# Writing out TensorE's order in the stage of four recurrent heads, with scans for window sums and a last tile in two pieces

## The chip, the core and the metric

The kernel runs on one core of one Trainium2 chip. The core has a matrix engine (TensorE, PE in the profile; PEld are its weight loads), a vector engine (VectorE, DVE), an activation engine (ScalarE, ACT), GpSimd (POOL) and SyncE (SP), which here only issues DMAs. Each engine works through its own queue in order, and engines wait for each other by semaphores. The metric is the time of one execution in microseconds (us), smaller is better. The kernel before takes 1327.94 us, the median of 3 runs (1326.75 to 1328.4).

## The reference, cut to what matters

One layer of a decoder trunk on 1024 tokens plus 16 meta tokens (L = 1040 rows) of width 1024, all in float32:

```python
u = rmsnorm(h, mix_norm_pre)
q, f_logit, i_in, g_out, v_pool, gate_a, gate_b = split(u @ w_in)
a = hgrn2(q, f_logit, i_in, g_out, lbs, hgrn_out_norm)      # 4 heads, key and value width 128
p = multiscale_pool(v_pool, pool_proj, pool_scale)          # 4 groups, windows 2, 4, 8, 16
z = sigmoid(gate_a) * (a @ w_branch_hgrn) + sigmoid(gate_b) * (p @ w_branch_pool)
h = h + rmsnorm(z @ w_out, mix_norm_post)
u = rmsnorm(h, ffn_norm_pre)
gt = causal_dwconv(u @ ffn_w_gate, ffn_conv_w, ffn_conv_b)
h = h + rmsnorm((gelu(gt) * (u @ ffn_w_up)) @ ffn_w_down, ffn_norm_post)
```

`hgrn2` is a linear recurrence per head: a state of 128 x 128 decays by a forget gate f for each key channel, takes in k times v, and is read by q. Its output is normalised per head by its root mean square, multiplied by a gain and by sigmoid(g). `multiscale_pool` takes, per group of 128 channels, the mean over the last w rows, less the row itself, through a 128 x 128 matrix and a scale.

## The kernel before, in words

Matmuls are done in three passes: each operand is split into a high and a low part (`hi`, `lo`: ACT rounds to fp32r, DVE subtracts), and high by high, low by high and high by low are summed. Splits are thus a large part of the work of ACT and DVE.

The stages in order of time: norms and the transposed features `uhi`/`ulo` (two large tiles, `ubig`, line 431); value and first gate projections; a Strassen stage for the logits f, for q and for the two branch gates, which go to DRAM; **the stage of the heads** (about 326 to 580 us), which the change is about; the output projection (`Mixer`); the gated MLP, again by Strassen; and the down projection with its own one-level Strassen scheme, whose last quarter of products is summed tile by tile at the end (lines 1725 to 1745).

The stage of the heads is described by the string `ORDER` (line 56). Its words are, in the order in which the program emits the work:

- `h0` to `h3`: the next step of that head's generator `head_steps` (line 650). A head has twelve steps. They are: load f, q, kb and k from DRAM; a block step (32-wide blocks on the diagonal, PE name `sb`, then the first growth); six levels 2, 4, ... 64 (PE name `sl`); the transposes of k (`pt`), ahead of which the head's values `vh` are loaded; the state chain (`ds`, then seven dependent DVE operations `st`); the output (`po`), its square and the split of the square (`rh` on ACT, `rl` on DVE); and the mean-square step (`ms`: a matmul with ones, then Ln and Exp on ACT, and two products on DVE with the gain and the gate `sg`).
- A level consists of small matmuls that read k and q, then `grow`, in which DVE multiplies halves of k and q by f in place, then a masked copy into `near` or copies by ACT into `sc`. The next level's matmuls need the grown k and q, and growth has to wait for the matmuls that read the old ones.
- `PV0` to `PV3` and `G2`, `G3`: projections of the features with 8 k (blocks of 128 input rows) in three chunks of columns, for the pool and for two output gates. `PVa1` and `PVb1` are the first and second half of `PV1`. `post_pv` copies the banks to `vp` and sums the windows by doubling: adds of the row and the row 1, 2, 4, 8 back (line 817), 1 + 2 + 3 + 4 = 10 adds for the four groups.
- `sp`: `pool_split`, which finishes the mean and splits it. `PP`: one k, the group's 128 x 128 matrix; `post_pp` writes `phi` (ACT) and `plo` (DVE).
- `BB0` to `BB7`, `BA0` to `BA7`: the branch projections of the pool and of the heads, 4 k each (PE names `pbb` and `pba`), multiplied by the gates loaded from DRAM (`sa`). `BB` reads all four `phi`/`plo`; `BA` reads all four heads' split outputs, which `sa` makes.
- `w0` to `w5`: weights of the MLP are loaded, split and stored to DRAM for later (`keep`, lines 911 to 931; DVE at lines 920 and 923).

A projection holds three PSUM banks from its first matmul until its results are copied out; there are eight banks. Most tiles of the stage live in 26 slots (`slot`, pool `fm`). Weights come through three raw buffers. DMAs on SP are issued in the order of the queue, and `issue_after` keeps a load behind an earlier one.

What sets the order: outside blocks marked `tc.manual_schedule(engines=...)`, a planner simulates the program when it is built and places each engine's instructions by the simulated times and by their place in the program. In such a block the engines that are named keep the written order. The loop over `ORDER` (lines 1139 to 1178) is in no such block: the planner orders all engines there, PE too, so what PE does in the profile is not the string word by word.

Of the kernel before, what the change touches and what calls it, by code (L numbers as in the profile page):

```python
# [14 lines left out]
P = 128  # L15
D = 1024
SEQ = 1024
NM = 16
# [48 lines left out]
def trunk_kernel(ctx: ExitStack, tc: tile.TileContext, x, meta_tokens, mix_norm_pre,  # L67
# [124 lines left out]
    def proj_parts(w, col, n_k, xs, chunks, ws=None, name="pj", by_bank=0):  # L192
# [5 lines left out]
        for k in range(n_k - by_bank):  # L198
            if 0 < k == n_k // 2:
                yield banks  # L200
# [449 lines left out]
    def head_steps(h):  # L650
# [70 lines left out]
        for lv in LEVELS:  # L721
            if lv == NM:
                pm = bank("sm")
                for i in range(HALO):
                    pe.matmul(pm[:NM, i : i + 1], k[:, i * NM : (i + 1) * NM], q[:, NM + T0 + i : NM + T0 + i + 1],
                              start=True, stop=True)
                act.copy(scm, pm[:NM, :HALO])
# [8 lines left out]
        heads[h]["v"] = slot(NCH * P, name="vh")  # L736
        vmeta = small([NM, P], "vmeta", "vmeta", 2)
        with tc.issue_after(stage["load"].ins):
            nc.sync.dma_start(vmeta, vmd[:, h * P : (h + 1) * P])
            nc.sync.dma_start(heads[h]["v"].rearrange("p (c v) -> p c v", c=NCH),  # L740
                              vd[:, :, h * P : (h + 1) * P].rearrange("c p v -> p c v"))
# [47 lines left out]
        rh, rl = split(rs, "r", eng(f"rsl.{h}"))  # L789
        yield  # L790
# [6 lines left out]
        dve.scalar_tensor_tensor(o, o, ong[:, h : h + 1], rs, ALU.mult, ALU.mult)  # L797
        eng(f"osg.{h}").tensor_tensor(o, o, sgs[h], ALU.mult)
# [6 lines left out]
    def post_pv(g, pv):  # L805
        w = POOL_WINDOWS[g]
        vp, s1 = slot(L, name="vp"), slot(L, name="s1")
        s2 = slot(L, name="s2") if w > 2 else None
        for (lo, n), ps in zip(CH_ALL, pv):
            act.copy(vp[:, lo : lo + n], ps[:, :n])  # L810
        cur, step = vp, 1
        bufs = [s1, s2]
        while step < w:
            nxt = bufs[0]
            bufs = bufs[::-1]
            a = 2 * step - 1
            dve.tensor_tensor(nxt[:, a:L], cur[:, a:L], cur[:, a - step : L - step], ALU.add)
            cur, step = nxt, 2 * step
        pooled[g] = (cur, vp)

    def pool_split(g):
        w = POOL_WINDOWS[g]
        cur, vp = pooled[g]
        if w > T0 + 1:

            c1 = small([P, 1], "c1", "c1", 2)
            dve.tensor_reduce(c1, vp[:, 0 : T0 + 1], mybir.AxisListType.X, ALU.add)
            dve.tensor_scalar(cur[:, T0 : T0 + 1], c1, float(w) / (T0 + 1), None, ALU.mult)
# [9 lines left out]
    def post_pp(g, pp):  # L838
        a, b_ = slot(TQ, F32R, "phi"), slot(TQ, F32R, "plo")
# [276 lines left out]
    jobs_ = [(k.rstrip("a"), i) for k, i in order if k[0].isupper() and k[-1] != "b"]  # L1116
# [22 lines left out]
    for kind, i in order:  # L1139
        if kind == "sp":  # L1140
            pool_split(i)
            continue
        if kind == "w":
            keep_first(i) if i < EARLY else next(keeps[i - EARLY])
            continue
        if kind == "sa":
            ahl[i] = split(heads[i]["o"], "a")
            continue
        if kind == "h":
            if i not in gens:  # L1150
                gens[i] = head_steps(i)
            next(gens[i], None)
            continue
        kind, part = kind.rstrip("ab"), kind[-1]
        src, n_k, xs, chunks, post = job(kind, i)
        if part == "b":
            banks = next(halves_of[kind, i])
# [3 lines left out]
            continue  # L1161
        if kind in ("BA", "BB"):
            load_gate(sas if kind == "BA" else sbs, kind == "BB", i)
        ws = loader.next()
        if (kind, i) == ("BA", KD - 1):
            z0 = [split_z(0, k) for k in range(ZA)]
        if part == "a":
            halves_of[kind, i] = proj_parts(None, 0, n_k, xs, chunks, ws=ws, name="p" + kind.lower())
            next(halves_of[kind, i])
            continue  # L1170
        banks = proj(None, 0, n_k, xs, chunks, ws=ws, name="p" + kind.lower(),
                     by_bank=2 if (kind, i) == ("BA", KD - 1) else 0)
        loader.ahead()
        pay()
        after[kind, i] = post(banks)
        if kind == "BA":
            dve.tensor_tensor(sas[i], sas[i], sbs[i], ALU.add)
            z[i] = sas[i]
# [546 lines left out]
    banks = [bank("pd") for _ in range(NT)]  # L1725
    for n, k in enumerate(range(KT, KH)):
        if n == 0:
            prep_last(KH - 2, False)
            for t in range(NT):
# [10 lines left out]
    for t in range(NT):  # L1740
        for j in range(KT):
# [34 lines left out]
```

## Time and profile before

| | before |
|---|---|
| median of 3 runs | 1327.94 us (1326.75 to 1328.4) |
| the profiled execution | 1327.77 us, its span 1326.0 us |
| mean granted clock of TensorE | 0.989 |
| ACT busy | 524.2 us (40%) |
| POOL busy | 356.7 us (27%) |

The profile was taken from one execution. Busy times are the unions of an engine's instructions; matmuls are pipelined and overlap, so the spacing of their starts, not the listed duration, tells what one costs. `x` counts instructions. The number in brackets behind an instruction is the idle time of its engine before it, and after `<-` what released it. In a group by line, the figures after `|` are the busy time in us and the mean in ns, then the idle time before. In a stretch, the last three columns are the granted clock of TensorE (1.00 is full speed), the share of the 16 DMA engines and GB/s.

### The profile page before, as it was taken

The page shows a single profiled execution, that of the slowest core. Times are in us where ns is not written, and L with a number is a line of the kernel's source. Part 1 is how long each engine was busy: PE and PEld are TensorE (multiplying, and loading weights), DVE is VectorE, ACT ScalarE, POOL GpSimd, SP SyncE. Part 2 cuts the span into 40 slices and gives each one's busy share as a digit, 9 for nine tenths or more (in the row PEclk, how much of TensorE's full clock was granted, in tenths as well). Part 3 has the DMA queues.
Part 4 walks back from the last instruction along what each step waited for, and adds up shares of the span by engine and source line. Part 5 has one row for each costly group of instructions (what it writes and reads, how often), then busy time and mean ns, then how long its engine had stood idle before and what let it go on. Part 6 is the DMA issues. An engine that isn't in the chain of part 4 may idle for free.

```text
span 1326.0 us, 21946 instructions
## 1 busy us (share of the span) xinstructions
PE 1292.2 (97%) x8617; PEld 1144.3 (86%) x8617; DVE 964.4 (73%) x1297; ACT 524.2 (40%) x903; POOL 356.7 (27%) x303
## 2 busy tenths in 40 slices
PE   8999999999988889999999999999999999999997
PEld 7799899999988789987898888888888888888886
DVE  6768965444677866775578999888998885455757
ACT  5554533333137444235564322222222233444443
POOL 3015333220000000061025555545555652000000
PEclk9999999999989989999999999999999999999999
DMA  7135643334341276887686677677767799666644
GB/s 273 42 106 175 198 147 104 112 109 144 121 151 49 79 248 230 311 279 258 229 286 234 180 208 191 191 207 176 174 157 165 162 250 304 216 223 222 222 174 159
DMA packets 143802, 247.62 MB, mean 187 GB/s; under 512 B 11000, under 2 KB 75164, under 8 KB 143698
## 3 DMA queue, kind: packets, MB, share of 16 engines
q1 hardware_dynamic: 131634, 221.83, 49.4%
q0 software_dynamic: 12064, 24.38, 11.0%
q8 instruction: 68, 1.11, 0.3%
q14 instruction: 36, 0.29, 0.1%
HBM read 174.11 MB, written 95.09 MB: 203 GB/s over the span
## 4 chain that ended last, share of the span: by engine, by line
PE 94%; issue 2%; ACT 2%; DMA 1%; DVE 1%; SPq 0%; DVEq 0%; ACTq 0%
PE P L303 17%; PE P L304 17%; PE P L306 17%; PE pd L183 5%; PE pd L184 5%; PE pd L185 5%; PE pm L183 2%; PE pm L184 2%; PE pm L185 2%; PE pbb L203 1%; PE pbb L204 1%; PE pbb L207 1%; PE pba L203 1%; PE pv L184 1%; PE pba L204 1%
## 5 line engine op out<-in xcount | busy, mean ns | idle before, releaser
L304 PE MATMUL P<-v,whi 128*128 128x512 f32 (+2 forms) x408 | 140.7, 353 | 0.0
L303 PE MATMUL P<-v,whi 128*128 128x512 f32 (+2 forms) x408 | 140.7, 352 | 0.0
L306 PE MATMUL P<-v,wlo 128*128 128x512 f32 (+2 forms) x424 | 135.1, 349 | 0.0
L274 POOL TENSOR_TENSOR swa<-wraw,wraw 128x512 f32<-128x512 f32 x32 | 51.0, 1595 | 190.7 <-DMA wraw<-in_w_in_dram 77.5
L248 ACT CAST whi<-wraw 128x512 fp32r<-128x512 f32 x90 | 53.1, 618 | 102.2 <-PE P L304 75.7
L1510 DVE TENSOR_TENSOR rot<-wraw,rot 128x1024 fp32r<-128x1024 f32 x31 | 38.0, 1224 | 72.3 <-ACT rot L1509 72.2
L303 PEld LDWEIGHTS P<-v,whi 128*128 128x128 f32 x408 | 76.7, 188 | 10.4
L304 PEld LDWEIGHTS P<-v,whi 128*128 128x128 f32 x408 | 76.6, 188 | 10.2
L306 PEld LDWEIGHTS P<-v,wlo 128*128 128x128 f32 x424 | 74.1, 188 | 10.8
L184 PE MATMUL pd<-rot 128*128 128x512 f32 x272 | 82.1, 389 | 0.0
L185 PE MATMUL pd<-rot 128*128 128x512 f32 x272 | 82.1, 389 | 0.0
L183 PE MATMUL pd<-rot 128*128 128x512 f32 x272 | 81.1, 389 | 0.1
L249 DVE TENSOR_TENSOR wlo<-wraw,whi 128x512 fp32r<-128x512 f32 x86 | 73.3, 875 | 2.7 <-ACT whi L248 2.7
L248 ACT CAST whi<-swa 128x512 fp32r<-128x512 f32 x64 | 38.1, 618 | 92.2 <-PE P L304 77.2
L249 DVE TENSOR_TENSOR wlo<-swb,whi 128x512 fp32r<-128x512 f32 x64 | 66.1, 1040 | 9.8 <-ACT whi L248 9.8
L1509 ACT CAST rot<-wraw 128x1024 fp32r<-128x1024 f32 x31 | 32.7, 1054 | 90.7 <-PE pd L185 89.4
L303 PE MATMUL P<-uhi,whi 128*128 128x258 f32 (+2 forms) x240 | 68.5, 303 | 0.0
L304 PE MATMUL P<-ulo,whi 128*128 128x258 f32 (+2 forms) x240 | 68.4, 303 | 0.0
L248 ACT CAST whi<-swb 128x512 fp32r<-128x512 f32 x64 | 38.2, 618 | 71.9 <-PE P L304 67.4
L303 PE MATMUL P<-t4h,whi 128*128 128x258 f32 (+2 forms) x228 | 65.5, 304 | 0.0
L303 PE MATMUL P<-t2h,whi 128*128 128x258 f32 (+2 forms) x228 | 65.3, 304 | 0.1
L304 PE MATMUL P<-t4l,whi 128*128 128x258 f32 (+2 forms) x228 | 65.3, 304 | 0.0
(380 smaller groups left out, 3841.1 us busy)
## 6 DMA issues: line engine op xcount, KB each, us to landing
wraw<-in_w_in_dram SPq DMA_DIRECT2D x36, 512.0 KB, 4.5
yt<-ysum SPq DMA_DIRECT2D x33, 512.0 KB, 5.5
wraw<-in_ffn_w_gate_dram SPq DMA_DIRECT2D x26, 512.0 KB, 5.8
wraw<-in_ffn_w_up_dram SPq DMA_DIRECT2D x22, 512.0 KB, 5.7
wsum<-in_ffn_w_down_dram SPq DMA_DIRECT2D x22, 512.0 KB, 8.4
wraw<-in_w_out_dram SPq DMA_DIRECT2D x18, 512.0 KB, 5.3
ysum<-ys SPq DMA_DIRECT2D x11, 768.0 KB, 6.1
sa<-sscr SPq DMA_DIRECT2D x16, 513.0 KB, 5.7
```

The costliest lines, as they stand in the source:

```text
L183: pe.matmul(ps, ahi, bhi, start=first, stop=False)
L184: pe.matmul(ps, ahi, blo, start=False, stop=False)
L185: pe.matmul(ps, alo, bhi, start=False, stop=last)
L203: pe.matmul(ps[:, :n], whi[:, k, :], xhi, start=(k == 0), stop=False)
L248: act.copy(hi, src)
L249: (pool_e if 4 <= i < 2 * self.early else dve).tensor_tensor(lo, src, rr(hi), ALU.subtract)
L274: pool_e.tensor_tensor(s1, a21, a22, ALU.add)
L303: pe.matmul(d, whi[:, k, :], xh[:, c : c + w], start=(k == 0 and onto is None), stop=False, **go)
L304: pe.matmul(d, whi[:, k, :], xl[:, c : c + w], start=False, stop=False, **go)
L306: pe.matmul(x[:, o : o + w], wlo[:, k, :], xh[:, c : c + w], start=False, stop=(k == 3), **go)
L1509: act.copy(hi, src)
L1510: dve.tensor_tensor(lo, src, rr(hi), ALU.subtract)
```

## The change

1. **PE's order.** The loop over the stage runs inside `tc.manual_schedule(engines={E.PE})`, so PE keeps the order of the string. The other engines are still planned.
2. **The string.** PV1 to PV3, G2 and G3 come in quarters of two k (p, q, r, s), the branch projections BB0 to BB6 in halves of two k (a, b), and one head's step, at times two, stands behind each. Heads 2 and 3, which went through their levels between G2 and PP3, now run on beside BB to its end; PP0 to PP3 stand behind the output step of head 0, around that of head 1.
3. **VLOAD.** The load of `vh` and `vmeta` is issued at level 8, four steps earlier.
4. **Scans.** The window sums of w = 4, 8, 16 are one `tensor_tensor_scan` each: a running sum that adds the row and subtracts the row w back. For that `vp` has 16 zero columns ahead of it, set by POOL. w = 2 keeps its one add. The special sum for row 14 goes.
5. **Pool outputs.** `phi` and `plo` (eight tiles) are written to one `ubig` tile, the place of the features, instead of eight slots.
6. **Gain and gate.** The product of a head's output with gain and gate is done ahead of the mean square, and one product is left behind it.
7. **Late end.** In the last products the fourth row tile is computed in two halves of 256 columns, with a bank of their own each. The first add to `c12` is moved ahead of a split. In the last loop ACT and DVE keep the written order, and the gain product is written to a tile of its own, `left`; before, it was written over the tile that the square reads.

The diff, cut to its core:

```diff
-ORDER = ("h0 h1 PV0 PVa1 h0 h1 PVb1 h0 h1 h0 PVa2 h1 sp0 h0 h1 PVb2 h0 h1 sp1 h0 h1 h2 PVa3 h0 h1 sp2 h0 h3 "
-         "PVb3 h1 h0 h1 h0 h1 h2 Ga2 sp3 h0 h1 h2 h3 Gb2 h2 h3 sa0 PP0 PP1 h2 h3 Ga3 h2 h3 h2 Gb3 h3 h2 h3 PP2 PP3 h2 h3 sa1 h2 h3 w0 w1 "
-         "BB0 w4 h2 h3 w4 BB1 h2 h3 BB2 sa2 h3 BB3 w5 BB4 sa3 w4 w5 BB5 w5 BB6 BB7 w5 BA0 w2 BA1 w3 BA2 BA4 BA3 BA5 BA6 BA7")
+ORDER = ("h0 h1 PV0 PVp1 PVq1 h0 PVr1 h1 PVs1 h0 PVp2 h1 PVq2 h0 sp0 PVr2 h1 PVs2 h0 PVp3 h1 sp1 PVq3 h0 PVr3 h1 "
+         "PVs3 h0 sp2 Gp2 h1 Gq2 h0 h2 Gr2 h1 Gs2 h0 sp3 Gp3 h1 h2 Gq3 h0 h3 Gr3 h1 h2 Gs3 h0 PP0 h2 PP1 h1 h3 PP2 "
+         "PP3 h0 h2 w0 w1 BBa0 w4 h3 BBb0 h1 h2 w4 sa0 BBa1 h3 BBb1 h2 sa1 BBa2 h3 h2 BBb2 h3 BBa3 h2 h3 BBb3 h2 w5 "
+         "BBa4 h3 BBb4 h2 h3 w4 w5 BBa5 h3 BBb5 h2 w5 h3 BBa6 h3 sa2 BBb6 h3 BB7 w5 sa3 BA0 w2 BA1 w3 BA2 BA4 BA3 "
+         "BA5 BA6 BA7")
+VLOAD = 8
...
-            if 0 < k == n_k // 2:
+            if k in cuts:
                 yield banks
...
         for lv in LEVELS:
+            if lv == VLOAD:
+                heads[h]["v"] = slot(NCH * P, name="vh")
+                vmeta = small([NM, P], "vmeta", "vmeta", 2)
+                with tc.issue_after(stage["load"].ins):
+                    nc.sync.dma_start(vmeta, vmd[:, h * P : (h + 1) * P])
+                    nc.sync.dma_start(heads[h]["v"].rearrange("p (c v) -> p c v", c=NCH),
+                                      vd[:, :, h * P : (h + 1) * P].rearrange("c p v -> p c v"))
...
         rh, rl = split(rs, "r", eng(f"rsl.{h}"))
+        dve.scalar_tensor_tensor(o, o, ong[:, h : h + 1], sgs[h], ALU.mult, ALU.mult)
         yield
...
-        dve.scalar_tensor_tensor(o, o, ong[:, h : h + 1], rs, ALU.mult, ALU.mult)
-        eng(f"osg.{h}").tensor_tensor(o, o, sgs[h], ALU.mult)
+        dve.tensor_tensor(o, o, rs, ALU.mult)
...
-        vp, s1 = slot(L, name="vp"), slot(L, name="s1")
-        s2 = slot(L, name="s2") if w > 2 else None
+        vz, cur = slot(NM + L, name="vp"), slot(L, name="s1")
+        vp = vz[:, NM:]
+        pool_e.memset(vz[:, :NM], 0.0)
...
-        while step < w:
-            nxt = bufs[0]
-            bufs = bufs[::-1]
-            a = 2 * step - 1
-            dve.tensor_tensor(nxt[:, a:L], cur[:, a:L], cur[:, a - step : L - step], ALU.add)
-            cur, step = nxt, 2 * step
+        if w == 2:
+            dve.tensor_tensor(cur, vp, vz[:, NM - 1 : NM - 1 + L], ALU.add)
+        else:
+            dve.tensor_tensor_scan(cur, vp, vz[:, NM - w : NM - w + L], 0.0, ALU.add, ALU.subtract)
...
-        a, b_ = slot(TQ, F32R, "phi"), slot(TQ, F32R, "plo")
+        if g == 0:
+            stage["phis"] = ubig(F32R, "phis")
+        a, b_ = (stage["phis"][:, (2 * g + i) * TQ : (2 * g + i + 1) * TQ] for i in range(2))
...
-    for kind, i in order:
+    with tc.manual_schedule(engines={E.PE}):
+        for kind, i in order:
...
     banks = [bank("pd") for _ in range(NT)]
+    pieces = [(banks[-1], slice(0, 256)), (bank("pd"), slice(256, 512))]
...
-        multiply(banks, held.pop(k), n == 0, False)
+        ops = held.pop(k)
+        multiply(banks, ops, n == 0, False, range(NT - 1))
+        multiply_pieces(ops, n == 0, False)
...
-        dve.tensor_tensor(c11[t], banks[t], c11[t], ALU.subtract)
-        half_norm(c11[t], t, 0)
-        finish(t, c11[t], c12[t])
+                dve.tensor_tensor(c11[t][:, n], ps[:, : n.stop - n.start], c11[t][:, n], ALU.subtract)
+                part = t == NT - 1 and i == 0
+                act.activation(junk[:, n], c11[t][:, n], AF.Square, accum_out=sums4 if part else ssq4[:, 0, t : t + 1])
+                dve.tensor_tensor(left[:, n], c11[t][:, n], g4[:, n], ALU.mult)
...
+            finish(t, left, c12[t])
```

More of the change, by code (lines that the diff above doesn't have):

```diff
@@ L190, in proj, with proj_parts @@
         return banks
-    def proj_parts(w, col, n_k, xs, chunks, ws=None, name="pj", by_bank=0):
+    def proj_parts(w, col, n_k, xs, chunks, ws=None, name="pj", by_bank=0, cuts=()):
         if ws is None:
@@ L734, in head_steps @@
             yield
[L736 to L741, printed above, removed]
         kt = slot(NCH * P, name="kt")
@@ L1114, in trunk_kernel @@
     open_pool("ps", 8, PSUM)
-    jobs_ = [(k.rstrip("a"), i) for k, i in order if k[0].isupper() and k[-1] != "b"]
+    jobs_ = [(k.rstrip("ap"), i) for k, i in order if k[0].isupper() and k[-1] not in "bqrs"]
     branch = [o_ for o_ in jobs_ if o_[0] in ("BA", "BB")]
@@ L1160, in trunk_kernel @@
             after[kind, i] = post(banks)
[L1161 to L1178, printed above, removed]
+            if kind == "BA":
+                dve.tensor_tensor(sas[i], sas[i], sbs[i], ALU.add)
+                z[i] = sas[i]
     if TRUNC:
```

86 lines of the change are left out of this document (59 added, 27 removed).

## The prediction

> **What bounds the kernel now.** I read the page's busy times first, then a table of stretches, then what TensorE (PE) waited for, then the waits instruction by instruction.
>
> ```profile
> span 1326.0 us, 21946 instructions
> ...
> PE 1292.2 (97%) x8617; PEld 1144.3 (86%) x8617; DVE 964.4 (73%) x1297; ACT 524.2 (40%) x903; POOL 356.7 (27%) x303
> ```
>
> PE is the bound: 1292.2 of 1326.0 us. The change takes no matmul away, so it can only win the 33.8 us in which PE is idle, and time in which it runs slowly. The table of stretches shows where these are. Columns: us, busy us of PE, its weight loads, VectorE (DVE), ScalarE (ACT), POOL, then the granted clock.
>
> ```profile
> 344.00:378.00 34.00, 27.79 (x817) 26.48 (x819) 27.16 (x45) 8.37 (x20) 0.35 (x2) 0.92 0.21 67
> 378.00:410.00 32.00, 30.31 (x233) 29.01 (x229) 22.07 (x44) 10.61 (x24) 0.60 (x4) 0.93 0.40 138
> 410.00:456.00 46.00, 39.04 (x879) 37.14 (x879) 34.97 (x59) 28.01 (x47) 1.91 (x2) 0.96 0.16 48
> 456.00:474.00 18.00, 11.31 (x100) 10.46 (x100) 14.26 (x29) 11.52 (x24) 0.00 (x0) 0.74 0.76 232
> 474.00:533.00 59.00, 59.00 (x390) 58.31 (x389) 38.77 (x62) 28.14 (x40) 0.00 (x0) 0.99 0.67 228
> ```
>
> From 344 to 474, in the stage of the heads, PE is idle for 6.21 + 1.69 + 6.96 + 6.69 = 21.5 us. From 474 to 533 the branch projections (pbb) run without a gap: the filler matmuls stand behind the stage that lacks them. The clock falls in four places of this stage. The table of these four, its first row and its sum:
>
> ```profile
> 355.20:358.60 3.40, 3.24 (x22) 3.21 (x23) 3.40 (x6) 0.00 (x0) 0.00 (x0) 0.54 0.36 106
> ...
> sum 23.80, PE 17.39 PEld 17.24 DVE 20.14 ACT 7.52 POOL 0.76; mean PE 4.35 PEld 4.31 DVE 5.03 ACT 1.88 POOL 0.19
> ```
>
> They last 23.8 us at about half clock, with PE busy for 17.39 us. At the full clock that work takes half the time: 8.7 us lost. What PE waits for in the stage (total, times, longest):
>
> ```profile
> PE ds L764 <- DMA vh<-vscr: 6.9, 2, 5.2
> PE sl L693 <- DVE q L676: 3.9, 2, 2.0
> PE sl L687 <- DVE q L676: 3.5, 2, 2.1
> ...
> PE sl L687 <- ACT sc L702: 1.9, 1, 1.9
> ```
>
> Apart from the load of the head's values (vh), these are chains: a level's matmuls, DVE's growth of k and q, the next level's matmuls, with too little between. PE's order shows it:
>
> ```profile
> 351.15 1.32 PE L693 MATMUL sl<-q,k 128*32 128x16 f32 x128
> 354.50 0.63 PE L693 MATMUL sl<-q,k 128*32 128x16 f32 x52 [2.03 <-DVE q L676]
> ...
> 367.55 0.32 PE L203 MATMUL ppv<-uhi,whi 128*128 128x346 f32 x1
> 367.80 0.74 PE L693 MATMUL sl<-q,k 128*32 128x16 f32 x64
> 368.47 0.43 PE L204 MATMUL ppv<-ulo,whi 128*128 128x346 f32 x1
> ```
>
> The levels of two heads run back to back (x128), and the next level has nothing ahead of it that is ready. At 367.8 a level stands in the middle of one k of a projection, which the written order does not ask for. So a planner sets PE's order here, and the edit that takes it away is a real one.
>
> **The change: PE's order.** In the chain of waits one k of a projection (three chunks) comes every 1.43 us:
>
> ```profile
> 327.76 0.48 PE ppv L207 x3
> 329.19 0.48 PE ppv L207 x3
> ```
>
> A level takes 0.7 us (the row at 367.8). A quarter of PV or G, or a half of BB, is two k, 2.87 us. In the new order two steps of one head have at least one such part and mostly a step of another head between them: 3.6 us, and often 6.4. A level's growth on DVE is q and k, then f and near on a half of the columns or fewer:
>
> ```profile
> L676 DVE TENSOR_TENSOR q<-q,f 128x512 f32<-128x512 f32 x24 | 16.4, 684 | 0.0
> L670 DVE TENSOR_TENSOR k<-k,f 128x528 f32<-128x528 f32 x16 | 11.3, 705 | 5.0 <-DMA k<-kscr 3.3 <-PE sl L693 1.7
> ```
>
> That is 0.68 + 0.71 and at most as much again by half, 2.1 us, inside 3.6 to 6.4. So the waits for q and sc go wherever DVE is behind by less than some 1.5 to 4 us. To be won at most: 21.5 of idle time and 8.7 of clock, 30.2 us. Now what is late next, at the places where I find DVE or ACT behind.
>
> (a) From PP0 to the first half of BB. PE has four PP of one k, two levels and head 3's block step (0.7 each), the output step of head 1 and the mean-square step of head 0:
>
> ```profile
> 480.26 0.38 PE L777 MATMUL po<-scm,vmeta 16*128 16x2 f32 x2
> ...
> 484.33 0.48 PE L757 MATMUL ds<-vmeta,ktm 16*128 16x128 f32 x2
> ...
> 492.14 0.64 PE L793 MATMUL ms<-rh,onesr 128*128 128x342 f32 x3
> ...
> 493.19 0.38 PE L777 MATMUL po<-scm,vmeta 16*128 16x2 f32 x2
> ```
>
> An output step is 4.1 us (480.26 to 484.33), a mean-square step 1.05 (492.14 to 493.19): in all 5.7 + 2.1 + 4.1 + 1.05 = 13.0 us. DVE has in the same time 12 plo, rl and the gain-and-gate product of two heads, head 3's first growth (four short ops and a long one), one level and two weight splits, which are as wide as rl:
>
> ```profile
> L842 DVE SCALAR_TENSOR_TENSOR plo<-ppp,par,phi 128x342 fp32r<-128x342 f32 x12 | 6.3, 567 | 0.0
> ...
> L797 DVE SCALAR_TENSOR_TENSOR o<-o,par,rs 128x1026 f32<-128x1026 f32 x4 | 5.2, 1290 | 8.1 <-ACT rs L796 8.1
> ...
> L835 DVE TENSOR_TENSOR rl<-rs,rh 128x1026 fp32r<-128x1026 f32 x4 | 4.9, 1229 | 4.6 <-ACT rh L834 4.6
> ```
>
> 6.3 + 2 x (1.23 + 1.29) + (2.1 + 1.23) + 2.1 + 2 x 1.23 = 19.2 us against 13.0. Most of these 6 us may lie later. What may not is the plo of PP2: PP2, PP3, the mean-square step and BB want three of the 8 PSUM banks each. Counted from the start of PP0, PE wants the third bank of the mean-square step after 1.4 + 0.7 + 1.4 + 4.1 + 0.7 + 2.9 + 0.7 = 11.9 us. DVE, in the written order, has the first plo of PP2 done after 0.5 (first chunk) + 1.6 (PP0) + 2.1 (level) + 2.5 (head 0) + 1.6 (PP1) + 3.3 (head 3) + 2.5 (head 1) + 0.5 = 14.6. I take 2.7 us of wait (bounds 0 and 6.2).
>
> (b) Head 3's end. Its mean-square step has only half of BB6 (2.87) between it and the output step. Head 2's output ended at 484.33, and its rl was done at 488.84:
>
> ```profile
> 487.61 1.23 DVE L835 TENSOR_TENSOR rl<-rs,rh 128x1026 fp32r<-128x1026 f32 x1 [0.26 <-ACT rh L834]
> ```
>
> That chain is 4.5 us long, so 1.6 stay open. What follows it (Ln, Exp, split) has the rest of BB and three k of BA0 over it, 2.87 + 5.73 + 4.3 us.
>
> (c) The kept FFN weights (w0, w1, w4, w5). Their work on DVE waits for loads and stores:
>
> ```profile
> L920 DVE TENSOR_TENSOR wlo<-wraw,wraw 128x512 f32<-128x512 f32 x6 | 4.0, 689 | 5.9 <-DMA kept7l<-wlo 2.6 <-DMA kept5l<-wlo 1.7 <-DMA wraw<-in_ffn_w_gate_dram 1.6
> ```
>
> Now these 5.9 us cost nothing, since pbb needs little of DVE. After the change the levels of heads 2 and 3 are queued behind these instructions on DVE, and PE waits for the levels. With a slack of 1.5 to 4 us at each I take half, 3 us (bounds 0 and 5.9).
>
> Waits left: 2.7 + 1.6 + 3 = 7.3 us. The gap of 2.03 us at 354.5 was followed by the 3.4 us at half clock in the table, 1.7 us lost; I take two such, 3.4. The Trainium skill, "TensorE: Matmul & The Clock Gate", Part 1, says that the clock falls after an idle window of about 3.4 us; by that rule gaps of 2 us cost no clock, and the time would be 3.4 us less. The 2.03 us gap disagrees, and the sum goes by it.
>
> **The other edits.** VLOAD: the load of vh is issued four steps earlier, on SP's queue ahead of the next head's loads, which are used 12 us later at the soonest. The longest wait for vh was 5.2 us; four steps are at least 4 x 3.6. So the 6.9 us go (counted above); if the cover fails, 5.2 come back. The pool outputs move to the space of the features, free once G3 is done, and G3 stands ahead of PP0 on PE: nothing new waits, and eight slots come free for the heads beside BB.
>
> Scans: nine adds of DVE go and three scans come.
>
> ```profile
> L817 DVE TENSOR_TENSOR s<-vp 128x1039 f32<-128x1039 f32 x4 | 5.0, 1246 | 0.6 <-ACT scm L727 0.6
> ```
>
> Nine times 1.25 are 11.2 us. No scan is in the trace; between one add (1.25) and two (2.5) each, DVE has 3.7 to 7.5 us less to do. This lies under PV, where DVE was busy for 27 of 34 us, so it adds slack to levels whose waits are counted already: nothing of its own. The small memsets go to POOL, busy for 2.9 of these 189 us. The gain-and-gate product is only moved ahead of the mean square.
>
> Late end. After the last matmul:
>
> ```profile
> 1319.04 0.69 DVE L1743 TENSOR_TENSOR acc<-pd,acc 128x512 f32<-128x512 f32 x1 [0.39 <-PE pd L185]
> 1319.76 0.63 ACT L1667 ACTIVATE junk<-acc 128x512 f32<-128x512 f32 x1 [3.03 <-DVE acc L1743]
> ...
> 1320.52 0.69 DVE L1668 TENSOR_TENSOR acc<-acc,g 128x512 f32<-128x512 f32 x1 [0.79 <-ACT junk L1667]
> ```
>
> Subtract and square on 256 columns save some 0.25 us each, and the gain, which no longer waits for the square, 0.3: 0.8 us won. Against it, 33 matmuls of 512 columns become 66 of 256:
>
> ```profile
> 1316.28 0.23 PE pd L183
> ```
>
> ```profile
> 324.95 0.28 PE L304 MATMUL P<-t4l,whi 128*128 128x258 f32 x1
> 325.07 0.28 PE L303 MATMUL P<-t4h,whi 128*128 128x256 f32 x1
> ```
>
> They start 0.12 us apart instead of 0.23: 33 x 0.01 to 0.02 is 0.3 to 0.6 us more. A ninth bank has to come free from c12's first add, up to 0.5. Together nothing (bounds -0.8 and +1.1).
>
> The profiled execution took 1327.77 us, its span and 1.8 around it, 0.2 below the median of 1327.94. 1327.8 - 30.2 + 7.3 + 3.4 = **1308.3 us**.
>
> **The rivals.** *All is covered:* (a) to (c) find slack, as most levels do. 1327.8 - 30.2 = 1297.6, or 1301 with one wait and its clock. For it: from 344 to 533 DVE has 137 us of work in 189, after the change some 132 in 159. Against it: (b) follows from the order alone. *The clock holds:* the same waits, none long enough to lower the clock: 1304.9. For it stands a wait after which no slow stretch came:
>
> ```profile
> 428.69 0.73 PE L693 MATMUL sl<-q,k 128*32 128x16 f32 x64 [2.13 <-issue]
> ```
>
> Against it stands the one at 354.5. This is what the rule of the page on the clock gate would give. *DVE becomes the bound beside BB:* heads 2 and 3 grow where DVE is busy for 38.8 of 59 us already. If (a) and (c) cost their upper ends (6.2 + 5.9), (b) 1.6, and four gaps 1.7 of clock each, 20.5 of the 30.2 come back: 1318. *PE blocked, slower:* in a fixed order PE cannot pass a late step. There are seven w4 and w5 steps, each with weights to load or buffers to get back from a store, and DVE's queue stands behind each. If each costs what the late vh cost, 5.2 us, and 1.7 of clock, that is 48 us: 1346. It turns slower from 30.2 / 6.9, at more than four such steps. Against it: the longest of these waits in (c) is 2.6 us. *Nothing changes:* DVE's work limits the stage as before, 1327; against it, vh is waited for while DVE is free.
>
> **Chances.** The forecast's case (1304 to 1312) 0.44, all covered 0.20, the clock holds 0.08, DVE the bound 0.14, nothing 0.06, slower 0.08. A difference of 0.2%, 2.7 us, is about what a measurement of this kernel can tell from none. Faster by more: 0.86; within it: 0.06; slower by more: 0.08. The range, 1297 to 1320, takes in all but the last two and the tails of the others.
>
> **What would show it.** Right: PE idle for about 7 us in the heads' stage; no wait of ds for vh; one head's level at a time between parts of projections; BA's projections starting some 20 us earlier; a wait of ms near head 3's end; nothing won or lost from there to 1300. Wrong: PE waiting in the chain for L920 or L923, a low clock beside pbb for more than two stretches, or more than 1 us either way after the last matmul.

## The result and the profile after

The changed kernel takes 1317.99 us, median of 4 runs (1316.83 to 1319.71). The kernel before, beside it on the same chip, takes 1327.67 (4 runs, 1326.75 to 1328.4). The ratio is 0.9933, 95% interval 0.9921 to 0.9946. So 9.7 us are won where 19.4 were forecast. The time lies inside the range, and the direction is right. The profiled execution took 1317.88 us.

The page of the kernel after, busy times:

```profile
span 1316.2 us, 21988 instructions
...
PE 1290.6 (98%) x8650; PEld 1139.7 (87%) x8650; DVE 961.2 (73%) x1293; ACT 522.5 (40%) x904; POOL 359.9 (27%) x307
```

PE is still the bound, with 25.6 us idle instead of 33.8. The table of stretches of the kernel after has the columns of the one before. Its first row is the whole stage of the heads, from the first matmul of PV to the first of BA. The next two are all the time at half clock in it, and then come the stretches used before:

```profile
326.20:521.78 195.58, 183.30 (x2505) 172.80 (x2505) 142.32 (x241) 89.61 (x161) 5.30 (x18) 0.97 0.52 168
425.40:428.90 3.50, 2.96 (x14) 2.99 (x15) 3.50 (x8) 1.33 (x4) 0.00 (x0) 0.53 0.28 109
439.00:446.00 7.00, 5.45 (x80) 5.42 (x81) 6.42 (x12) 6.69 (x9) 0.00 (x0) 0.52 0.61 203
344.00:378.00 34.00, 34.00 (x780) 31.78 (x769) 27.96 (x42) 7.10 (x14) 0.00 (x0) 1.00 0.15 38
378.00:410.00 32.00, 32.00 (x343) 30.09 (x339) 19.96 (x36) 12.26 (x30) 1.88 (x6) 1.00 0.41 134
410.00:456.00 46.00, 37.94 (x586) 35.27 (x587) 33.35 (x59) 28.29 (x48) 1.05 (x2) 0.89 0.58 186
456.00:474.00 18.00, 16.35 (x320) 15.26 (x320) 18.00 (x36) 7.82 (x15) 0.00 (x0) 1.00 0.62 207
474.00:533.00 59.00, 56.43 (x418) 54.03 (x417) 41.18 (x72) 33.09 (x53) 0.00 (x0) 1.00 0.69 228
```

The same stage in the kernel before:

```profile
326.58:532.49 205.91, 184.37 (x2504) 178.10 (x2505) 144.21 (x244) 88.99 (x159) 5.05 (x14) 0.94 0.46 151
```

From 344 to 410 PE is busy for all of 66 us, where it had been idle for 7.9. Most of what is left sits in one place, from 410 to 456: 8.1 of the 12.3 us that PE is idle in the stage, and both slow stretches. The stage is 10.3 us shorter (205.9 to 195.6), and that splits into three:

| in the stage, us | before | forecast | after |
|---|---|---|---|
| PE idle | 21.5 | 7.3 | 12.3 (195.58 - 183.30) |
| lost to the low clock | 8.7 | 3.4 | 4.2 (half of 2.96 + 5.45) |
| the rest: PE's own time at full clock | 175.7 | 175.7 | 179.1 |

What the forecast missed here is thus 5.0 of waits, 0.8 of clock and 3.4 of PE's own time, 9.2 in all. The waits of PE after, one by one (those over 1 us, and the 0.42 us that belongs to the last):

```profile
425.94 0.76 PE L788 MATMUL po<-sc,vh 128*128 128x128 f32 x2 [2.00 <-DVE near L711]
...
438.14 0.42 PE L798 MATMUL ms<-rh,onesr 128*128 128x342 f32 x1 [2.55 <-DVE phis L842]
...
440.55 1.06 PE L696 MATMUL sl<-q,k 128*32 128x16 f32 x64 [1.83 <-ACT rs L800]
...
453.00 0.73 PE L696 MATMUL sl<-q,k 128*32 128x16 f32 x64 [1.51 <-DVE near L711]
...
466.88 1.12 PE L690 MATMUL sl<-q,k 128*64 128x64 f32 x16 [1.65 <-DVE q L679]
...
510.81 0.42 PE L798 MATMUL ms<-rh,onesr 128*128 128x342 f32 x1 [0.42 <-ACT rh L832]
...
512.41 0.43 PE L799 MATMUL ms<-rl,onesr 128*128 128x342 f32 x1 [1.18 <-DVE rl L833]
```

Place (a) of the prediction is the first three: 6.4 us against 2.7. Place (b) is the last two: 1.6 against 1.6. Place (c) is the two in between, levels behind the kept weights: 3.2 against 3.0. Some 1.1 lie elsewhere. So of the 5.0 us of waits that the forecast missed, 3.7 are in (a). No matmul waits for `vh`.

The 2.00 us come out of DVE's queue. DVE of the kernel after:

```profile
421.45 0.29 DVE L153 TENSOR_TENSOR wlo<-wraw,whi 128x128 fp32r<-128x128 f32 x1 [3.78 <-PE ppp L210]
423.09 1.29 DVE L794 SCALAR_TENSOR_TENSOR o<-o,par,sg 128x1026 f32<-128x1026 f32 x1 [1.34 <-ACT phis L841]
424.29 0.70 DVE L673 TENSOR_TENSOR k<-k,f 128x528 f32<-128x528 f32 x1
424.91 0.68 DVE L679 TENSOR_TENSOR q<-q,f 128x512 f32<-128x512 f32 x1
425.51 0.28 DVE L711 COPY_PREDICATED near<-mask,sl 128x128 f32<-128x128 uint8 x1
```

The second row is the product with gain and gate that edit 6 moved ahead of the mean square. The releaser named, `phis` on ACT, does not feed it. It reads the gate `sg`, whose load SP issued only 3.4 us before and whose last completion the trace has at 423.01; the square of the same output, which the product must not overtake, had ended at 422.17:

```profile
419.73 0.34 SPq L779 DMA_DIRECT2D sg<-gscr  x1
```

Behind it in DVE's queue stands head 2's growth with `near`, which frees a bank that the output of head 1 (`po`) wants. A product that nobody needs before the mean square is done holds up PE.

The same kind of row carries the first half of place (c), the 1.51 us, in the kernel after:

```profile
449.99 1.29 DVE L920 TENSOR_TENSOR wlo<-wraw,wraw 128x512 f32<-128x512 f32 x2 [3.59 <-DMA wraw<-in_ffn_w_gate_dram]
451.20 0.70 DVE L673 TENSOR_TENSOR k<-k,f 128x528 f32<-128x528 f32 x1
451.82 0.69 DVE L679 TENSOR_TENSOR q<-q,f 128x512 f32<-128x512 f32 x1
452.42 0.43 DVE L711 COPY_PREDICATED near<-mask,sl 128x128 f32<-128x128 uint8 x1
```

DVE stands for 3.59 us before a split whose weights are still on their way, with a level's growth behind it. The second half, the 1.65 us at 466.88, is of another kind: DVE does not stand still there, it is busy for all of the 18.00 us from 456 to 474 (the table above), and two splits of kept weights (1.2 us) are part of that work ahead of the level's growth. In this short stretch DVE is short of time.

Behind the stage some 0.9 us are lost. One wait of 1.2 us is new (552.17, BA for `sa`). At the end, PE's last matmul starts at 1318.61 of 1326.0 before and at 1309.53 of 1316.2 after, so that tail is 0.7 shorter; the smaller matmuls ahead of it take that back.

### The profile page after: what moved, and what is told of

It is laid out like the page before. It is cut to its first block, busy times and chain, and to the rows that moved or that the text cites. A ratio compares the mean times of both kernels' runs of the same rounds, so it can differ in the third digit from the quotient of the medians.

```text
span 1316.2 us, 21988 instructions
## 1 busy us (share of the span) xinstructions
PE 1290.6 (98%) x8650; PEld 1139.7 (87%) x8650; DVE 961.2 (73%) x1293; ACT 522.5 (40%) x904; POOL 359.9 (27%) x307
## 4 chain that ended last, share of the span: by engine, by line
PE 91%; DVE 3%; DMA 2%; ACT 2%; issue 1%; SPq 0%; DVEq 0%; ACTq 0%
PE P L306 17%; PE P L307 17%; PE P L309 17%; PE pd L186 5%; PE pd L188 5%; PE pd L187 5%; PE pm L186 2%; PE pm L188 2%; PE pm L187 2%; PE ppv L206 1%; PE ppv L210 1%; PE pg L206 1%; PE ppv L207 1%; PE pv L187 1%; PE pv L186 1%
## 5 line engine op out<-in xcount | busy, mean ns | idle before, releaser
L252 DVE TENSOR_TENSOR wlo<-wraw,whi 128x512 fp32r<-128x512 f32 x86 | 76.4, 911 | 2.7 <-ACT whi L251 2.7
```

The lines of the kernel that those rows point to most:

```text
L252: (pool_e if 4 <= i < 2 * self.early else dve).tensor_tensor(lo, src, rr(hi), ALU.subtract)
```

## The experiments

Theory 1: what is lost against the forecast comes from the *order* in which DVE gets its work between PP0 and the middle of BB (the early product, the splits of the kept weights), and from a price that PE pays at each return from a projection to a head's step. Theory 2: DVE is simply short of time beside BB, so work that is put elsewhere comes back as another wait. Each ratio is to runs of the kernel before beside it on the same chip; over a whole set of such runs its median was 1327.1 to 1327.6. Differences from the kernel after are differences of medians across chips; some tenths of a us in them mean nothing.

**gain_back: the product behind the mean square again.**

```diff
         rh, rl = split(rs, "r", eng(f"rsl.{h}"))
-        dve.scalar_tensor_tensor(o, o, ong[:, h : h + 1], sgs[h], ALU.mult, ALU.mult)
         yield
...
-        dve.tensor_tensor(o, o, rs, ALU.mult)
+        dve.scalar_tensor_tensor(o, o, ong[:, h : h + 1], rs, ALU.mult, ALU.mult)
+        dve.tensor_tensor(o, o, sgs[h], ALU.mult)
```

> The changed kernel with one edit undone: the gain-and-gate product of a head's output is again behind the mean square. Theory 1 (the order of DVE's queue between PP0 and the first part of BB makes the waits there, and the moved product waits for the gate's load ahead of head 2's growth): the 2.0 us for which head 1's output step waits go, and up to 1.7 us of clock with them; 2 to 4 us faster than the changed kernel, 1314 to 1316. Theory 2 (DVE simply has too much to do beside PP and BB, whatever the order): another wait takes its place, 1317 to 1319.

1316.15 us, ratio 0.9917 (0.9901 to 0.9934). This lies just above the 1314 to 1316 of theory 1, and its interval overlaps that of the kernel after (0.9921 to 0.9946), so the time alone shows no gain. The trace says more. DVE's growth of head 2:

```profile
422.28 0.71 DVE L673 TENSOR_TENSOR k<-k,f 128x528 f32<-128x528 f32 x1 [0.32 <-PE sl L696]
```

It starts 2.0 us earlier than after (424.29), and `po` no longer waits, nor does the level that had waited 1.83. But DVE then reaches the kept weights' split earlier too and waits there, and the waits of PE that lead this kernel's list are now

```profile
PE sl L696 <- DVE near L711: 3.6, 1, 3.6
PE pbb L206 <- ACT rs L799: 2.7, 2, 2.2
PE ms L797 <- DVE phis L842: 1.9, 1, 1.9
```

The first of them is place (c), with 3.6 instead of 1.5. The second, BB waiting for banks of a mean-square step, is 0.2 in the kernel after. So the moved product is the cause of the 2.00 us, and it hid a part of (c). That other waits take the place of the one removed is what theory 2 expected, and in the whole stage PE's idle time falls only from 12.3 to 11.2 us.

**pairs: the steps of heads 0 and 1 back to back, with two quarters behind both.**

```diff
-... PVp1 PVq1 h0 PVr1 h1 PVs1 h0 PVp2 h1 PVq2 h0 sp0 PVr2 h1 PVs2 h0 PVp3 h1 sp1 PVq3 h0 PVr3 h1
-    PVs3 h0 sp2 Gp2 h1 Gq2 h0 h2 Gr2 h1 Gs2 ...
+... PVp1 PVq1 h0 h1 PVr1 PVs1 h0 h1 PVp2 PVq2 h0 sp0 h1 PVr2 PVs2 h0 h1 PVp3 sp1 PVq3 h0 h1 PVr3 PVs3
+    h0 sp2 h1 Gp2 Gq2 h0 h2 h1 Gr2 Gs2 ...
```

> The changed kernel, with the steps of heads 0 and 1 from the block step to level 64 one right behind the other and two quarters behind both, so that PE changes between projections and small matmuls seven times less. Theory 1 adds that each return from a head's step to a projection costs PE some 0.15 to 0.2 us (a quarter takes 3.06 us in the trace, 2.87 without interruption): the stretch from the first block step to the first transposes, 52.8 us without a wait, gets 1.0 to 1.4 us shorter, with no wait in it, and the time about 1 us less, 1317. Theory 2: the growth of both heads comes at once, DVE is late, and waits of 1 us and more appear at the levels: 1319 and more.

1317.24 us, ratio 0.9928 (0.9912 to 0.9944): in the time, not to be told from the kernel after. The stretch itself can be compared, since PE has no wait in it in either kernel. PE after:

```profile
343.55 0.76 PE L719 MATMUL sb<-q,kb 128*32 128x32 f32 x64
...
347.29 0.76 PE L719 MATMUL sb<-q,kb 128*32 128x32 f32 x64
347.98 0.43 PE L206 MATMUL ppv<-uhi,whi 128*128 128x348 f32 x1
...
351.04 0.74 PE L696 MATMUL sl<-q,k 128*32 128x16 f32 x64
...
396.37 1.03 PE L751 MATMUL pt<-ident,k 128*128 128x128 f32 x8
```

PE of pairs:

```profile
343.67 1.36 PE L715 MATMUL sb<-q,kb 128*32 128x32 f32 x128
344.96 0.42 PE L202 MATMUL ppv<-uhi,whi 128*128 128x348 f32 x1
...
394.47 0.71 PE L747 MATMUL pt<-ident,k 128*128 128x128 f32 x5
```

From the first block step to the first transposes after takes 52.8 us and pairs 50.8, with 7 returns fewer: 0.29 us each. The rows show the same price in the small: the quarter from 347.98 to 351.04 takes 3.06 us, 0.19 more than the 2.87 of two k at 1.43, and two block steps of 64 matmuls take 0.69 each (347.29 to 347.98), 0.09 more together than the 1.29 of both in one run (343.67 to 344.96). From the first matmul of PV to the first of BA there are 24 unbroken runs of projection matmuls before and 36 after. Twelve more at 0.29 are 3.5 us, and PE's own time grew by 3.4. That product is an estimate, and the count alone does not set PE's own time: pe_written_alone, below, has 16 runs, 8 fewer than before, and pe_planned 41, but their own times, worked out as in the table above, are 175.4 and 178.5 us, much as before and after. The 2.0 us won in this stretch mostly do not reach the end; among the later waits, that of BA for `sa` is 1.9 instead of 1.2.

**pe_planned: the kernel after, with PE planned.**

```diff
-    with tc.manual_schedule(engines={E.PE}):
+    if True:
         for kind, i in order:
```

> The changed kernel without the block that keeps PE's order; the new string and all the other edits stay. If the string makes the gain, the planner finds nearly the same order: within 2 us of 1318. If the fixed order makes it, the planner puts levels back to back again and waits of 2 us with low clock return under PV and G: 1322 to 1328. Both theories leave this open; my guess is 1322.

1318.97 us, ratio 0.9938 (0.9922 to 0.9955), not to be told from the kernel after. The waits have other names (this kernel's list):

```profile
PE ms L798 <- ACT rs L800: 5.0, 1, 5.0
PE ms L798 <- ACT rh L832: 2.8, 1, 2.8
```

**pe_written_alone: the kernel before, with its old string in the written order on PE.**

```diff
-    for kind, i in order:
+    with tc.manual_schedule(engines={E.PE}):
+        for kind, i in order:
```

> The kernel before, with one edit only: PE keeps the written order of the old string. The old string has two steps of one head with nothing but the other head's step between them at several places, and heads 2 and 3 go through their levels around four PP and two G: the waits stay or grow, 1325 to 1340, if the string is what counts (both theories). If the planner's swaps made the waits, 1315 to 1320.

1327.71 us, ratio 1.0007 (0.9996 to 1.0018): nothing. The waits in its list are those of before:

```profile
PE ds L764 <- DMA vh<-vscr: 6.2, 2, 4.9
PE sl L687 <- DVE q L676: 4.3, 3, 2.1
PE sl L693 <- DVE q L676: 4.3, 3, 2.0
```

In both strings, whether PE's order is fixed or planned makes no difference that these runs can measure.

**keep_late: the kept weights later, much of `w4` and `w5` beside BB7 and BA.**

```diff
-... h2 w0 w1 BBa0 w4 h3 BBb0 h1 h2 w4 sa0 ... BBb3 h2 w5 BBa4 ... w4 w5 BBa5 h3 BBb5 h2 w5 h3 ... BB7 w5 sa3 BA0 w2 BA1 w3 BA2 BA4 BA3
+... h2 BBa0 h3 BBb0 h1 h2 sa0 ... BBb2 w0 w1 ... BBb3 h2 w4 ... BBb4 h2 h3 w4 BBa5 ... BBb6 h3 w4 BB7 w5 sa3 BA0 w5 BA1 w5 BA2 w5 BA4 w2 BA3 w3
```

> The changed kernel with only the w words of the string moved back: w0 and w1 behind BBb2, w4 behind BBb3, BBb4 and BBb6, all w5 into BA, so that the growth of heads 2 and 3 no longer stands behind DVE instructions that wait for these loads. Theory 1: the waits of the levels on near (1.5 us) and on q (1.65) beside BB go, the waits between PP0 and BB (2.0, 2.55, 1.83) stay: 2.5 to 4 us faster than the changed kernel, 1314 to 1315.5. Theory 2 (the amount of DVE's work is the bound): other waits of the same sum appear, 1317 to 1319, or BA waits for its gates' products, slower.

1319.57 us, ratio 0.9953 (0.9939 to 0.9966): slower than forecast. Place (c) is empty, as theory 1 says: no level beside BB waits, and BA begins at 519.5 instead of 521.8. But the weights are now late for the stage behind. PE of keep_late, at the start of the output projection:

```profile
570.19 0.50 PE L182 MATMUL pm<-whi,zc 128*128 128x512 f32 x1 [1.39 <-ACT whi L1218]
...
572.62 0.80 PE L183 MATMUL pm<-wlo,zc 128*128 128x512 f32 x1 [1.93 <-POOL wlo L1220]
```

3.3 us of waits and a stretch of 6.8 us at half clock there (571.3 to 578.2) take it back.

**ms_later: head 0's mean-square step behind the first half of BB0.**

```diff
-... PP3 h0 h2 w0 w1 BBa0 w4 h3 ...
+... PP3 h2 w0 w1 BBa0 h0 w4 h3 ...
```

> The changed kernel with head 0's mean-square step moved behind the first half of BB0. Theory 1 (PP2, PP3, the mean-square step and BB want twelve banks, and DVE frees them late): the wait of ms on phis (2.55) and of the level on Ln (1.83) are replaced by one shorter wait of BB0, 1 to 2.5 us; with the stretch at half clock behind them (6.8 us) shortened by half: 2 to 5 us faster, 1313 to 1316. Theory 2: BB0 waits as long as ms did, 1317 to 1319.

1322.28 us, ratio 0.9970 (0.9961 to 0.9979), 4 to 5 us slower than after. The list of waits of this kernel begins:

```profile
PE pbb L202 <- ACT rs L796: 3.2, 1, 3.2
PE pbb L202 <- DVE phis L838: 2.7, 1, 2.7
PE po L784 <- DVE near L707: 2.1, 1, 2.1
```

Now BB waits for `plo` (2.7) instead of the mean-square step (2.55), and a second time for banks that the mean-square step holds until Ln. The banks are wanted by whoever comes next. My theory 1 expected a gain here and was wrong: this wait comes from how late `plo` is, not from who stands behind it.

**vload_back: the values' load at the transposes again.**

```diff
         for lv in LEVELS:
-            if lv == VLOAD:
-                heads[h]["v"] = slot(NCH * P, name="vh")
-                ... (the loads)
...
+        heads[h]["v"] = slot(NCH * P, name="vh")
+        ... (the loads)
         kt = slot(NCH * P, name="kt")
```

> The changed kernel with the load of a head's values back ahead of the transposes of k, where it was before. If the earlier load took away the waits for vh (6.9 us and their clock), they return, at least for heads 2 and 3, where SP's queue holds the kept weights: 5 to 10 us slower, 1323 to 1328. If the new string alone took them away, since a quarter and more now lies between the transposes and the state chain: 1318.

1322.32 us, ratio 0.9969 (0.9958 to 0.9981): 4 to 5 us slower than after. Its list of waits has one for the load, that of head 3:

```profile
PE ds L767 <- DMA vh<-vscr: 3.6, 1, 3.6
```

So of the 6.9 us that were put down to edit 3 alone, the new string removes about half by itself, and the early load the rest with the clock behind it: this run has two more stretches of 3.4 us at half clock (from 500.7 and from 517.8) than the kernel after.

**end_alone: the kernel before with the late end** (edit 7 as in the diff above).

> The kernel before with only the late end: the fourth row tile in two pieces, the gain product to its own tile, the written order on ACT and DVE. From the trace of the changed kernel, from the end of the last matmul to the end of the span 0.6 us less, and 33 matmuls as 66 shorter ones 0.4 us more: 0.2 us faster, which can't be told from none, 1326.5 to 1328.5. Theory 2 says nothing of it.

1326.35 us, ratio 1.0000 (0.9991 to 1.0008): nothing, as forecast.

**string_and_place: the kernel before with edits 2 and 5 alone**, the new string and the pool outputs in the place of the features. PE is planned, and values, adds, products and end are as before. The string is tried with edit 5 because it keeps more tiles alive at a time than the 26 slots hold with `phi` and `plo` among them.

> The kernel before with two edits only: the new string, and the pool outputs in the features' place (without that place the new string has more tiles alive than there are slots). PE is planned, values are loaded late, sums by adds, product and end as before. If the string carries the gain, 1318 to 1322, with the wait for vh still in it. If the other edits carry it together, 1325 to 1328.

1323.58 us, ratio 0.9976 (0.9966 to 0.9987): 3.5 us won, between the two ranges that were expected. So string and place carry a part of the gain, and not the whole; the two were not tried apart. One wait for `vh` of 2.6 us is in it, as expected. The largest wait on its list is a single one, of a level:

```profile
PE sl L696 <- ACT rs L798: 8.1, 1, 8.1
```

**scans_back: the kernel after with the doubling adds.**

```diff
...
-        if w == 2:
-            dve.tensor_tensor(cur, vp, vz[:, NM - 1 : NM - 1 + L], ALU.add)
-        else:
-            dve.tensor_tensor_scan(cur, vp, vz[:, NM - w : NM - w + L], 0.0, ALU.add, ALU.subtract)
+        while step < w:
+            nxt = bufs[0]
+            ...
+            dve.tensor_tensor(nxt[:, a:L], cur[:, a:L], cur[:, a - step : L - step], ALU.add)
...
```

> The changed kernel with the window sums by adds again. Scans measured 2.31 us each, so nine adds (11.2 us) cost DVE 4.3 us more than three scans (6.9). Under PV PE had no wait and DVE was busy for 28 of 34 us. Theory 1: that slack hides it, within 1.5 us of the changed kernel, 1317 to 1319. Theory 2 (amount of DVE's work): 3 to 4 us slower, 1321 to 1322.

1321.28 us, ratio 0.9956 (0.9941 to 0.9971): about 3 us slower than after, though the two intervals still touch (0.9921 to 0.9946). The time fits theory 2, but the trace does not show DVE as the cause. Under PV, the place of these adds, PE waits once, and for nothing that the profile can name (PE of scans_back):

```profile
376.59 0.32 PE L206 MATMUL ppv<-uhi,whi 128*128 128x348 f32 x1 [1.70 <-issue]
```

With a wait of 2.3 instead of 1.2 for `sa` in BA, that accounts for 2.8 us. Why PE stood there stays open. A 16 KB packet of the DMA queue for instructions is under way from 374.13 to 375.23, just where the gap begins; whether PE waited for it is not shown.

**keep_mid: the kept weights a little later, but done by BB7.**

```diff
-... h2 w0 w1 BBa0 w4 h3 BBb0 h1 h2 w4 sa0 BBa1 h3 BBb1 h2 ... BBb2 h3 BBa3 h2 h3 BBb3 h2 w5 BBa4 ... BBa6 h3 sa2 BBb6 h3 BB7 w5 sa3
+... h2 BBa0 h3 BBb0 h1 h2 sa0 BBa1 h3 BBb1 w0 w1 h2 ... BBb2 w4 h3 BBa3 h2 h3 BBb3 h2 w4 BBa4 ... BBa6 h3 sa2 BBb6 h3 w5 BB7 w5 sa3
```

> The changed kernel with the w words only a little later: w0 and w1 behind BBb1, w4 behind BBb2, BBb3 and BBb4, all w5 done before BA as in the changed kernel. The run with all of them late showed no wait of a level beside BB, but 3.3 us of waits and a low clock where the output projection begins. Theory 1: both are avoided, waits of 2.0, 2.55 and 1.83 between PP0 and BB and of 1.6 at head 3's end stay: 1314.5 to 1316. Theory 2: the same sum of waits elsewhere, 1318 or more.

1315.76 us, ratio 0.9912 (0.9897 to 0.9927). The waits of levels for `near` and `q` beside BB are gone, and what heads the list is place (a):

```profile
PE ms L794 <- DVE phis L838: 2.6, 1, 2.6
PE po L784 <- DVE near L707: 2.2, 1, 2.2
```

Two later waits have grown, though: the output of head 3 waits 2.0 us for `sa` on DVE (0.6 after) and a state chain 1.4 for `kt` on ACT (0.4 after). PE is idle for 11.7 us of the stage against 12.3, so most of the 3.2 us of place (c) came back elsewhere, as theory 2 expected; BA's wait of 1.2 for `sa` is gone too, and the time lies where theory 1 had it.

**mended: pairs, keep_mid, and the early product only for heads 2 and 3.**

```diff
+        if h >= EARLY_G:
+            dve.scalar_tensor_tensor(o, o, ong[:, h : h + 1], sgs[h], ALU.mult, ALU.mult)
         yield
...
+        if h >= EARLY_G:
+            dve.tensor_tensor(o, o, rs, ALU.mult)
+        else:
+            dve.scalar_tensor_tensor(o, o, ong[:, h : h + 1], rs, ALU.mult, ALU.mult)
+            dve.tensor_tensor(o, o, sgs[h], ALU.mult)
```

(The two lines of the kernel after go, and the string has the edits of pairs and of keep_mid.)

> Three things together on the changed kernel: the steps of heads 0 and 1 in pairs up to level 64 (2.0 us of PE's own time in that run's trace), the early product only for heads 2 and 3, whose gates are on the chip (2.0 us of wait went), and the w words a little later (3 us of waits). Theory 1: the parts add up, as they lie at different places: 1309 to 1313. Theory 2: DVE's work is the bound and only its place moves: 1315 to 1318.

1310.41 us (1308.71 to 1310.94), ratio 0.9871 (0.9855 to 0.9888). It beats the kernel before by 17 us and the kernel after by 7 to 8. BA begins at 515.3. The stretch from 410 to 456, where the kernel after has PE busy for 37.94 us, in mended:

```profile
410.00:456.00 46.00, 42.86 (x711) 39.68 (x709) 38.40 (x68) 31.96 (x54) 1.05 (x2) 0.93 0.52 167
```

and the list of its waits begins:

```profile
PE ms L795 <- DVE phis L843: 1.9, 1, 1.9
PE pbb L202 <- ACT rs L797: 1.3, 1, 1.3
PE ms L796 <- DVE rl L834: 1.0, 1, 1.0
```

DVE does *more* in that stretch than after (38.40 us against 33.35), and PE waits less. The same stretch holds somewhat other work in the two kernels, so the whole stage, from the first PV to the first BA, is the better comparison: DVE has as much to do (141.0 us against 142.3) in 189.1 us instead of 195.6, and PE is idle for 6.9 us instead of 12.3. The amount of DVE's work thus does not bound the stage at its length after. So theory 1 holds for the greater part: each of its edits takes its own wait away, and together they give more than any alone. Theory 2 has a part as well: alone, gain_back and keep_mid got much of their waits back elsewhere, ms_later handed the wait on, and keep_late gave it to a later stage. For place (a) theory 2 is not refuted: `plo` stays late whatever was tried.

## Why the prediction was right and wrong

**Right: where the time is, and the direction.** All the gain lies in the stage of the heads: 10.3 us of the stage, against 9.7 in the end. PE's idle time there fell from 21.5 to 12.3, BA begins 10.7 us earlier, and one head's level at a time stands between parts of projections. The waits of levels for `q` in PV and G are gone altogether.

**Wrong: "the gain-and-gate product is only moved ahead of the mean square".** The move was costed at nothing. The product's length stood in the sum of DVE's work for place (a), but put behind head 2's growth and with no wait of its own. In the trace it stands ahead of that growth and waits for the gate's load. In place (a) it cost 2.0 us of PE's time at 425.9, by its own wait of 1.34 and its length of 1.29. gain_back shows it. The next wait of (a) is the one that the prediction named, for `plo` of the pool outputs: 2.55 against 2.7. The wait of 1.83 behind it, of a level for the mean square's bank, was not in the sum; gain_back has 0.5 in its place, of BB. So (a) came to 6.4 us, just over its upper bound of 6.2.

**Wrong: PE's own time was taken as unchanged.** A quarter was priced at 2.87 us and a level at 0.7, as if they could be cut apart at no cost. PE's own time came out 3.4 us longer. A return from a head's step to a projection costs, and pairs puts the price of one more at 0.29 us; twelve of them would be 3.5. The price is shown for the seven of pairs. That it makes up the whole 3.4 is an estimate, which pe_written_alone, with fewer runs of projections and the same own time as before, does not bear out. The row for it stood in the prediction: the first matmul of a run at 367.8 is a level in the middle of a k, and its neighbours' starts were not set against 1.43.

**Right: places (b) and (c).** 1.6 against 1.6 and 3.2 against 3. (c) was half of two bounds, so its size owes something to luck. Its mechanism, growth in DVE's queue behind splits that wait for their loads, is what the rows at 449.99 show for the 1.51 us; the 1.65 us come with a DVE that is busy without a gap.

**The clock: nearly right, by a rule that does not hold.** 4.2 us against 3.4. In the kernel after, both slow stretches come with a gap of 2 us or more (2.00, then 2.55 with 1.83 close behind), and after the single gaps of 1.51 and 1.65 the clock stays at full speed. This goes against the Trainium skill, "TensorE: Matmul & The Clock Gate", Part 1, by whose idle window of about 3.4 us taken alone none of these gaps would have cost any clock. But the prediction's own row, a gap of 2.03 us that costs 1.7, is no rule either: in the kernel before, the gap of 2.13 us (428.69) left the clock at full speed, as did one of 1.99 in keep_mid (502.54), while mended has a stretch of 3.4 us at half clock from 505.8 about gaps of only 0.60 and 0.96 (503.04 and 504.42). What decides was not separated, so that the number of slow stretches was right owes something to luck.

**The rival that named the time.** "DVE becomes the bound beside BB" was put at 1318, which is what was measured. Its (a), 6.2, is near the 6.4, but it had 5.9 in (c) and 6.8 of clock where 3.2 and 4.2 came, and PE's own time as unchanged. Its number is thus luck in part; of its mechanism the runs show the one level at 466.88.

**Edit 1 carries nothing that can be told.** The prediction called it "a real one" because PE's order in the trace was not the string's. pe_written_alone and pe_planned show that fixing the order is worth nothing measurable in either string. What carries the gain: the string with the place for it (3.5 alone), the early values (4 to 5, taken out of the whole) and the scans (about 3, taken out of the whole, by a cause left open). These were measured in different company, so they do not have to add up to 9.7. That the first two are worth more than nothing is shown; for the scans the intervals touch.

**The scans: right on the size, open on the worth.** One scan takes 2.31 us, between the bounds of 1.25 and 2.5 (group of the kernel after):

```profile
L819 DVE TENSOR_TENSOR_SCAN s<-vp 128x1040 f32<-128x1040 f32 x3 | 6.9, 2309 | 0.0
```

Against 11.2 for nine adds, DVE has 4.3 us less to do. The Trainium skill, "DVE: opcode table, instruction layouts, handler registers and perf-mode slots", section 6, has the scan at half throughput; the trace agrees, with 2.31 against 1.25 for an add. "Nothing of its own" was the price in the prediction, and scans_back took 3 us more.

**The late end: right.** 0.7 us won in the tail against 0.8, given back ahead of it, and nothing in end_alone.

## What to carry to other kernels

When a step moves within an engine's queue, cost its inputs as well as its length: a product that is ready late costs the engine's whole queue its wait, though nobody needs the product itself. Filler cut into finer parts has a price per cut, so put no more cuts than the chain between them needs. And before a waiting step is moved, ask what else wants the same bank or buffer: twice here, the wait only changed its owner.

## What the runs showed of the hardware

- A return of PE between projections (128 x 128 weights, 342 to 348 columns) and a head's levels and block steps (32 columns of weights, 16 to 32 moving) costs some 0.29 us beyond the matmuls themselves: in pairs, 7 fewer saved 2.0 us. Of this, 0.19 us lie within the projection's quarter and 0.09 in the small matmuls; what it consists of was not separated.
- TensorE's granted clock fell to about half for 3.4 to 7 us about gaps of 2.0 to 2.6 us in the kernel after, and not about its single gaps of 1.51 and 1.65. The length of a gap does not decide alone: 2.13 us in the kernel before and 1.99 in keep_mid left the clock at full speed, and 0.60 and 0.96 close together in mended did not (0.50 from 505.8).
- A wait put down to "issue" can be as long as 2.13 us in the kernel before (428.69) and 1.70 in scans_back (376.59), with no releaser shown.
- Where the releaser named for a DVE product was an instruction on ACT that does not feed it (423.09 in the kernel after), the load that it reads had completed 0.08 us before: a named releaser is to be checked against what the instruction reads.
